# First output projection with three column groups over all token blocks and the fourth by pairs; the later modulation summed during it; gate rows made ahead

## The chip, the cores and the metric

The kernel runs on one core of one Trainium2 chip. The metric is the device time of one execution in microseconds (us); for the kernel before the change it is the median of three runs. TensorE does the matrix products (PE in the profile, PEld for its weight loads), VectorE (DVE) and ScalarE (ACT) the elementwise work, SyncE (SP) issues all DMA transfers from one queue in order.

## What is computed

Two layers over 512 tokens of width 2048, all float32. Each layer normalises, modulates with `1 + scale` and `shift`, mixes, normalises the mixer's output, scales it with `gate` and adds it to the stream. Shift, scale and gate come from one vector `c` through a large matrix product.

```python
for l in range(DEPTH):
    mod = sc @ ada_w[l] + ada_b[l]          # sc = silu(c); 2048 x 6144 per layer
    shift, scale, gate = mod[:, :D_MODEL], mod[:, D_MODEL:2 * D_MODEL], mod[:, 2 * D_MODEL:]
    h = modulate(rmsnorm(x, g_pre[l]), shift, scale)
    if l < N_A_LAYERS:
        y = mlstm_mixer(h, a_w_in[l], ..., a_w_out[l])
    else:
        if l == N_A_LAYERS:
            kmod = sc @ kv_ada_w + kv_ada_b
            hkv = modulate(rmsnorm(x, kv_g), kmod[:, :D_MODEL], kmod[:, D_MODEL:])
            kv = hkv @ kv_w
            ...
        y = band_attention_mixer(h, k_sh, v_sh, b_w_in[j], b_rel[j], b_w_out[j])
    x = x + gate[:, None, :] * rmsnorm(y, g_post[l])
```

## The kernel before

Everything is one Tile program, `hybrid_trunk`. It writes the work in program order; a scheduler that runs when the program is built sets each engine's order from priorities and its own estimate of times, and hands out the buffers of a pool as they come free in that order. Every engine and the SP queue then run strictly in the order so fixed. `tc.high_priority(AHEAD)` moves instructions ahead of program order, `pin` keeps instructions in program order among themselves.

**Products in three passes.** A float32 operand is split into a high part (ACT, a cast) and the rest (DVE, a subtraction), and each product is three matmuls (`mm3`, L280). Weights come as a stream of pieces that `stream` (L75) lists and `raw_load`/`wpiece` (L223, L232) load, 512 KB for a piece of 128 x 1024, and split on L213; three raw pieces and three split ones are held. `proj_b` (L299) takes pieces of two rows of blocks by 512 columns: with four token blocks a piece feeds 24 matmuls, with a pair of token blocks 12. Its argument `at` holds steps that are written into the program ahead of a given row of blocks.

**Layer 0, front (L816 to L949).** A loop over eight heads. The modulation that layer 0's gate and the key input need, 48 columns of blocks, is summed in the background of heads 0 to 2: `background(n)` (L743) sums what it loaded the time before on DVE (L507, 128 x 2048 elements, 1 MB of `adaT` each) and loads n more into two buffers (`ada_load`, L501). For head 0 it stands at rows 2, 4, 8, 10 and 14 of the value projection, for head 1 at 2, 6, 8 and 12, for head 2 after each of four projections. `gates` (L678) and `scores` (L785) are other DVE work of head 0. Each head's output goes to DRAM (`ysc`).

**Layer 0, output projection (L1100 to L1115).** `rows(g, ms, ...)` (L1065) multiplies by columns g of `a_w_out`: group 0 for all four token blocks, then groups 1 to 3 for token blocks 0 and 1, then groups 1 to 3 again for blocks 2 and 3, so that these weights are loaded and split twice. `evac` (L993) multiplies the result with a row of gates from `gate_row` (L989) and sums its squares (`sqy`). While the second pair runs, the first is finished: `residual(m)` (L1010) loads x (`xr`, four tiles of pool `tp`), adds, stores the new stream (`xsc`) and sums squares (`sqx`); `turned(pair, gs, use)` (L1030) scales (`xn`, DVE), transposes on TensorE (`ps_x`, L1046), copies (`xk`, ACT) and stores the turned stream (`nsc`); if `use` it also makes the key input from PSUM (`key_input`, L1022: one ACT operation, then a split). For the first pair `use` is False: the key input is made later, in group 3, from tiles loaded back (`kept`, L1056). In the background, `scale_sums` and `scale_load` (L1076, L1084) sum the shift and scale of layer 1, 32 columns of blocks in quarters of 512 elements (128 loads of 256 KB, four buffers). Pool `tp` has six tiles of 256 KB, pool `rp`, which holds the projection's results, twelve.

**Keys and values (L1118 to L1195).** `values` (L1118) first runs for the pair 0 on groups 0 and 1, with `residual(2)` and `residual(3)` written ahead of it, `scale_steps(4, 10)` in group 0 and `turned(1, ...)` in group 1, at rows 2, 6, 10 and 14; then for pair 1, with `input_sums`. Eight pairs of key tiles follow (`proj_s`), with the rest of the scale sums, then `values` for groups 2 and 3.

**Layer 1.** Attention (L1302 to L1332), then the output projection `b_w_out` (L1402): three groups for all token blocks, the last by pairs. The sixteen columns of layer 1's gate are summed here, in halves of 1024 elements: `gate_sums` (L1381) at eight steps, four loads of 512 KB and four sums each, with four buffers. Four times, `gate_part` turns four of the columns into gate rows (`gates_out`, L756, one TensorE transpose `ps_gg` each) and stores them; `gate_row` loads a row just before it is needed; group 0 is multiplied last (`gate_first`).

Of the kernel before, what the change touches and what calls it, by code (L numbers as in the profile page):

```python
# [9 lines left out]
F32 = mybir.dt.float32  # L10
# [64 lines left out]
def stream():  # L75
# [81 lines left out]
def hybrid_trunk(ctx, tc, xT, xN, c, adaT, cols, wst, wg, ext, kc, out):  # L157
# [658 lines left out]
    for h in range(NH):  # L816
# [4 lines left out]
        for i in range(4):  # L821
# [10 lines left out]
            if 1 < h <= HALF:  # L832
                background(2)
# [21 lines left out]
        if h < HALF:  # L855
            add_at(at, {k: lambda: background(2) for k in ((2, 4, 8, 10, 14) if h == 0 else (2, 6, 8, 12))})
# [103 lines left out]
    tp = tst.enter_context(pool("t2", bufs=6, side="right"))  # L960
# [28 lines left out]
    def gate_row(layer, g, gb=ssum):  # L989

        nc.sync.dma_start(gb, ggd[layer, 4 * g : 4 * g + 4, :].rearrange("k p -> (k p)").partition_broadcast(P))

    def evac(ps, m, g, dst, gated=True, later=None):  # L993
        if later is not None:
            later[m] = lambda: nc.vector.tensor_tensor(dst, ps, gb, op=ALU.mult)
        elif gated:
            nc.vector.tensor_tensor(dst, ps, gb, op=ALU.mult)
        else:
            nc.vector.tensor_copy(dst, ps)
# [30 lines left out]
    def turned(pair, gs, use):  # L1030
# [3 lines left out]
        for g in gs:  # L1034
# [5 lines left out]
            for kk in range(2):  # L1040
# [24 lines left out]
    def rows(g, ms, xs, at={}):  # L1065
# [7 lines left out]
    scale_cols = [(48 + i, j) for j in range(4) for i in range(2 * KT)]  # L1073
    scale_in, scQ = [], []

    def scale_sums():  # L1076

        for i, j, a in scale_in:
            pin(nc.vector.tensor_tensor_reduce(  # L1079
                a, a, scQ[j], 1.0, mod[:, i : i + 1] if j else col(CB + i), ALU.mult, ALU.add, mod[:, i : i + 1]  # L1080
            ))
        scale_in.clear()

    def scale_load():  # L1084

        for i, j in scale_cols[:2]:
            d = slice(j * S, (j + 1) * S)
            if len(scQ) == j:
                scQ.append(cp.tile([P, S], F32, tag="sc", name=f"scQ{j}", bufs=2))
                pin(nc.sync.dma_start(scQ[j], csc[0, d].partition_broadcast(P)))  # L1090
            a = cp.tile([P, S], F32, tag="adq", name=f"adq{i}_{j}", bufs=4)
            pin(nc.sync.dma_start(a, adaT[i, :, d]))
            scale_in.append((i, j, a))
        del scale_cols[:2]

    def scale_steps(*ks):
        at = {k: lambda: (scale_sums(), scale_load()) for k in ks}
        return at | {k + 2: scale_load for k in ks}

    gate_row(0, 0)  # L1100
    rows(0, range(4), y_tile, scale_steps(4, 10, 16, 22, 28))
    for pair, ms in enumerate(PAIRS):
        for g in range(1, 4):
            at = scale_steps(4, 12, 20, 28) if pair == 0 else {}
            if pair == 1 and g == 1:
                at = {2: lambda: residual(0), 4: lambda: residual(1)}
                at |= {20 + 4 * i: lambda i=i: turned(0, [i], False) for i in range(3)}
            if pair == 1 and g == 2:
                at = {2: lambda: turned(0, [3], False)}
            if pair == 1 and g == 3:  # L1110
                at = {k: lambda k=k: [key_input(i, kept(i, slice(0, 2 * P)), slice(0, 2 * P)) for i in range(k // 2 - 1, k // 2 + 1)] for k in range(2, 32, 4)}
            if pair == 1:
                add_at(at, scale_steps(*((8, 14), (6, 14, 22), (8, 20))[g - 1]))
            gate_row(0, g)
            rows(g, ms, ys, at)  # L1115
# [46 lines left out]
    for pair, ms in enumerate(PAIRS):  # L1162
        for g in range(2):
            turn = {2 + 4 * i: lambda i=i: turned(1, [i], True) for i in range(4)} if pair == 0 and g == 1 else {}
# [10 lines left out]
    for i in range(KT // 2):  # L1175
# [3 lines left out]
        if 0 < i < 7:  # L1179
            add_at(at, {1: lambda: (scale_sums(), scale_load()), 3: scale_load})  # L1180
        if i == 7:
            at[1] = lambda: (scale_sums(), amul_cols(2, 48 + KT, GPRE + KT))
# [3 lines left out]
    assert not scale_cols and not scale_in  # L1186
# [5 lines left out]
    for g in range(2, 4):  # L1192
        n = -(-ATT_PAIRS // 2)
        ks = [k for k in range((g - 2) * n, min((g - 1) * n, ATT_PAIRS))]
        values(g, range(4), {2 + 4 * i: input_sums for i, k in enumerate(ks)})  # L1195
# [175 lines left out]
    late, last = [], {}  # L1371
    gate_cols = [(80 + i, j) for i in [*range(4, KT), *range(4)] for j in range(2)]
    gate_in = []

    def gate_begin():
        late.append(op.tile([P, D], F32, tag="sc", name="scC", bufs=1))
        late.append(op.tile([P, S], F32, tag="gb", name="gb0", bufs=1))
        nc.sync.dma_start(late[0], csc.rearrange("a d -> (a d)").partition_broadcast(P))
        gate_sums()

    def gate_sums():  # L1381

        for a in gate_in:
            ada_sum(*a, tc.keep_in_program_order, late[0])
# [86 lines left out]
```

## Time and profile before

| what | us |
|---|---|
| median of three runs | 2764.67 |
| lowest and highest run | 2760.27, 2767.65 |
| the profiled execution's own time | 2763.39 |
| its span, first to last instruction | 2761.6 |
| mean granted TensorE clock in it | 0.998 of full speed |

The profile is one execution, in microseconds from the first instruction. "Busy" is the time in which an engine's instructions ran; a matmul's end is modelled and its record overlaps the next, so the pace of TensorE is read from the number of matmuls in a stretch. A row of waits names the waiting instruction, `<-`, what it waited for, the sum of the waits, their number and the longest one. A row of the timeline gives start, duration, engine, line, operation, written tile `<-` read tiles, count, and in brackets the idle time before it. `SPq` is the issue of a DMA on SyncE's queue. In windows each engine's busy time is followed by its number of instructions, and at the end stand the granted TensorE clock, the busy share of the 16 DMA engines and their rate.

### The profile page before, as it was taken

What the parts mean: (1) busy time and instruction counts of PE and PEld (TensorE: products, weight loads), DVE (VectorE), ACT (ScalarE), POOL (GpSimd) and SP (SyncE); (2) the same over time, 40 slices, a digit from 0 to 9 for tenths busy, and PEclk for the clock granted to TensorE, in tenths of its full rate; (3) what the DMA queues carried; (4) which work ended last, traced back from release to release, by engine and by line L of the source; (5) the groups of instructions that cost most, each with busy time, mean ns of one, the idle gap of its engine ahead of it and who ended that gap; (6) DMA issues with size and microseconds to landing.
All of it is one profiled execution on the core that took longest, in us unless ns stands there. A gap on an engine that the chain in (4) does not pass through costs nothing.

```text
span 2761.6 us, 45211 instructions
## 1 busy us (share of the span) xinstructions
PE 2730.8 (99%) x17554; PEld 2486.7 (90%) x17554; DVE 2327.1 (84%) x3822; ACT 1440.0 (52%) x2048; POOL 0.2 (0%) x4
## 2 busy tenths in 40 slices
PE   8999999999999999999999999999999999999998
PEld 6887888899999999999998888877998999999887
DVE  8977979999899899998988577667996798898666
ACT  4243623555556565565555344558435566666523
POOL 0000000000000000000000000000000000000000
PEclk9999999999999999999999999999999999999999
DMA  9756787333333333333338699998655544444697
GB/s 368 290 205 222 265 327 273 121 100 125 107 111 114 95 123 108 115 110 100 125 107 282 215 295 304 303 308 272 216 178 192 168 122 130 127 125 130 211 313 238
DMA packets 174802, 527.27 MB, mean 191 GB/s; under 512 B 18757, under 2 KB 34661, under 8 KB 163961
## 3 DMA queue, kind: packets, MB, share of 16 engines
q1 hardware_dynamic: 174586, 524.38, 56.7%
q8 instruction: 137, 2.24, 0.3%
q14 instruction: 79, 0.65, 0.1%
HBM read 490.69 MB, written 38.85 MB: 192 GB/s over the span
## 4 chain that ended last, share of the span: by engine, by line
PE 79%; DVE 9%; DMA 8%; issue 2%; ACT 1%; SPq 0%; DVEq 0%; ACTq 0%
PE ps_y L278 11%; PE ps_azo L278 5%; PE ps_czo L278 5%; PE ps_dzo L278 5%; DMA ada<-in_adaT 4%; PE ps_kv L278 4%; PE ps_az L278 3%; PE ps_cz L278 3%; PE ps_dz L278 3%; PE ps_l L278 3%; PE ps_bzo L278 3%; DVE wl L213 3%; PE ps_o L278 3%; PE ps_v L278 2%; DVE ada L507 2%
## 5 line engine op out<-in xcount | busy, mean ns | idle before, releaser
L213 ACT CAST wh<-wr 128x1024 fp32r<-128x1024 f32 (+1 forms) x560 | 579.6, 1037 | 531.2 <-PE ps_y L278 185.9
L213 DVE TENSOR_TENSOR wl<-wr,wh 128x1024 fp32r<-128x1024 f32 (+1 forms) x560 | 673.5, 1205 | 177.8 <-ACT wh L213 175.3
L278 PE MATMUL ps_y<-wh,y 128*128 128x512 f32 x1536 | 476.5, 390 | 0.0
L213 ACT CAST wsh<-ws 128x768 fp32r<-128x768 f32 (+1 forms) x272 | 222.5, 818 | 416.4 <-PE ps_az L278 123.2
L278 PEld LDWEIGHTS ps_y<-wh,y 128*128 128x128 f32 x1536 | 288.1, 188 | 59.3
L213 DVE TENSOR_TENSOR wsl<-ws,wsh 128x768 fp32r<-128x768 f32 (+1 forms) x272 | 254.4, 935 | 85.9 <-ACT wsh L213 82.7
L278 PE MATMUL ps_y<-wl,y 128*128 128x512 f32 x768 | 299.6, 390 | 0.1
L507 DVE CUSTOM_DVE_ANT_0 ada<-ada,scB,cl 128x2048 f32<-128x2048 f32 (+1 forms) x80 | 185.5, 2320 | 20.1 <-DMA ada<-in_adaT 19.9
L252 DVE TENSOR_TENSOR ws<-wr 128x512 f32<-128x512 f32 (+1 forms) x272 | 181.7, 673 | 2.7 <-DMA wr<-in_wst 2.6
L278 PEld LDWEIGHTS ps_y<-wl,y 128*128 128x128 f32 x768 | 144.2, 188 | 31.3 <-DVE wl L213 1.8
L278 PE MATMUL ps_kv<-wh,hkv 128*128 128x512 f32 x512 | 160.5, 393 | 0.0
L278 PE MATMUL ps_v<-wh,h 128*128 128x512 f32 x384 | 120.2, 390 | 0.0
L278 PEld LDWEIGHTS ps_kv<-wh,hkv 128*128 128x128 f32 x512 | 96.9, 190 | 19.9
L254 DVE TENSOR_TENSOR ws<-wr 128x256 f32<-128x256 f32 (+1 forms) x272 | 111.6, 415 | 2.7
L253 DVE TENSOR_TENSOR wr<-ws,wr 128x256 f32<-128x256 f32 (+1 forms) x272 | 111.2, 414 | 1.8
L278 PE MATMUL ps_kv<-wl,hkv 128*128 128x512 f32 x256 | 101.3, 396 | 2.3 <-DVE wl L213 2.3
L278 PE MATMUL ps_l<-h,wh 128*128 128x512 f32 x320 | 98.4, 390 | 0.0
L278 PEld LDWEIGHTS ps_v<-wh,h 128*128 128x128 f32 x384 | 72.0, 188 | 14.8
L278 PE MATMUL ps_azo<-h,wh 128*128 128x256 f32 (+1 forms) x404 | 82.1, 294 | 0.0
L278 PE MATMUL ps_v<-wl,h 128*128 128x512 f32 x192 | 75.0, 391 | 0.0
L1079 DVE CUSTOM_DVE_ANT_0 adq<-adq,scQ,mod 128x512 f32<-128x512 f32 x96 | 69.6, 747 | 5.8 <-DMA adq<-in_adaT 5.8
L278 PEld LDWEIGHTS ps_l<-h,wh 128*128 128x128 f32 x320 | 59.9, 188 | 12.7 <-ACT wh L213 0.3
(442 smaller groups left out, 7242.3 us busy)
## 6 DMA issues: line engine op xcount, KB each, us to landing
wr<-in_wst SPq DMA_DIRECT2D x530, 512.0 KB, 4.1
ada<-in_adaT SPq DMA_DIRECT2D x78, 1024.0 KB, 6.7
adq<-in_adaT SPq DMA_DIRECT2D x128, 256.0 KB, 5.1
ada<-in_adaT SPq DMA_DIRECT2D x36, 512.0 KB, 7.2
xt<-nsc SPq DMA_DIRECT2D x48, 256.0 KB, 4.6
wr<-in_wst SPq DMA_DIRECT2D x26, 384.0 KB, 3.2
yr<-ysc SPq DMA_DIRECT2D x28, 256.0 KB, 5.3
ysc<-zo SPq DMA_DIRECT2D x24, 256.0 KB
```

What stands on the lines that cost most here:

```text
L213: ins = nc.scalar.copy(hi, src), nc.vector.tensor_tensor(lo, src, hi.bitcast(F32), op=ALU.subtract)
L252: nc.vector.tensor_tensor(t[:, : 2 * w], r[:, w : 3 * w], r[:, : 2 * w], op=ALU.subtract)
L253: nc.vector.tensor_tensor(r[:, w : 2 * w], t[:, w : 2 * w], r[:, :w], op=ALU.add)
L254: nc.vector.tensor_tensor(t[:, 2 * w :], r[:, 3 * w :], r[:, w : 2 * w], op=ALU.subtract)
L278: return nc.tensor.matmul(ps, a, b, start=start, stop=stop)
L507: pin(nc.vector.tensor_tensor_reduce(c, c, (sc or scB)[:, j * w : (j + 1) * w], 1.0, mod[:, i : i + 1] if j else col(CB + i), ALU.mult, AL ...
L1079: pin(nc.vector.tensor_tensor_reduce(a, a, scQ[j], 1.0, mod[:, i : i + 1] if j else col(CB + i), ALU.mult, ALU.add, mod[:, i : i + 1]))
```

## The change

The first output projection goes through its column groups 0, 1 and 2 for all four token blocks, and only through group 3 by pairs, so that 80 pieces of weights are loaded and split where there were 112. The key input of pair 0 is made straight from PSUM in `turned`, as it was for pair 1, and the reload (`kept`) of that pair goes. All modulation of layer 1, gate columns too, is summed during this projection and the key tiles, in halves of 1024 elements, two loads of 512 KB and two sums a step, with two buffers: a step at every fourth row of group 0, at every second row but the last of groups 1 and 2, and at four rows of the first pair of group 3. The eight steps of the last projection and its four transposes go; one `gates_out` for all sixteen columns stands in `values` of group 2. Two results of pair 0 live in pool `tp`, which gets a seventh tile. In layer 0's front, head 0 has seven background steps in its value projection in place of five, head 1 three in place of four, and head 2 loads six columns in place of eight.

```diff
-    tile_b("a_w_out", 0, 32)
-    for _ in PAIRS:
-        for g in range(1, 4):
-            tile_b("a_w_out", g * 512, 32)
+    for g in (0, 1, 2, 3, 3):
+        tile_b("a_w_out", g * 512, 32)
...
             if 1 < h <= HALF:
-                background(2)
+                background(2 - i % 2)
...
-            add_at(at, {k: lambda: background(2) for k in ((2, 4, 8, 10, 14) if h == 0 else (2, 6, 8, 12))})
+            add_at(at, {k: lambda: background(2) for k in ((2, 4, 6, 8, 10, 12, 14) if h == 0 else (2, 6, 12))})
...
-    tp = tst.enter_context(pool("t2", bufs=6, side="right"))
+    tp = tst.enter_context(pool("t2", bufs=7, side="right"))
...
-                if use:
-                    for j in range(2):
-                        key_input(k + j, ps[:, j * 2 * P : (j + 1) * 2 * P], t)
+                for j in range(2):
+                    key_input(k + j, ps[:, j * 2 * P : (j + 1) * 2 * P], t)
...
-                yt[m].append(rp.tile([P, S], F32, tag="r", name=f"y{m}_{g}"))
+                yt[m].append((pl or rp).tile([P, S], F32, tag="t" if pl else "r", name=f"y{m}_{g}"))
...
+    cols_left = [(48 + i, j) for j in range(2) for i in range(2 * KT)] + [(80 + i, j) for j in range(2) for i in range(KT)]
+    halves, sc = [], [None, None]
+    def half_sums_step():
+        for i, j, a in halves:
+            pin(nc.vector.tensor_tensor_reduce(
+                a, a, sc[1], 1.0, mod[:, i : i + 1] if j else col(CB + i), ALU.mult, ALU.add, mod[:, i : i + 1]
+            ))
+        halves.clear()
+        for i, j in cols_left[:2]:
+            d = slice(j * 2 * S, (j + 1) * 2 * S)
+            if sc[0] != j:
+                sc[:] = j, cp.tile([P, 2 * S], F32, tag="sc", name=f"scH{i}_{j}")
+                pin(nc.sync.dma_start(sc[1], csc[0, d].partition_broadcast(P)))
+            a = cp.tile([P, 2 * S], F32, tag="adh", name=f"adh{i}_{j}", bufs=2)
+            pin(nc.sync.dma_start(a, adaT[i, :, d]))
+            halves.append((i, j, a))
+        del cols_left[:2]
...
     gate_row(0, 0)
-    rows(0, range(4), y_tile, scale_steps(4, 10, 16, 22, 28))
-    for pair, ms in enumerate(PAIRS):
-        for g in range(1, 4):
-            at = scale_steps(4, 12, 20, 28) if pair == 0 else {}
...
-            gate_row(0, g)
-            rows(g, ms, ys, at)
+    rows(0, range(4), y_tile, steps_at(*range(2, 32, 4)))
+    for g in (1, 2):
+        gate_row(0, g)
+        rows(g, range(4), ys, steps_at(*range(0, 30, 2)))
+    gate_row(0, 3)
+    rows(3, PAIRS[0], ys, steps_at(2, 10, 18, 26), tp)
+    at = {2: lambda: residual(0), 4: lambda: residual(1)}
+    at |= {14 + 4 * i: lambda i=i: turned(0, [i]) for i in range(4)}
+    rows(3, PAIRS[1], ys, at)
...
-            elif g == 0:
-                turn = scale_steps(4, 10)
...
+        if i == 0:
+            amul_cols(2, 48 + KT, GPRE + KT)
+        if 0 < i:
+            at[1] = half_sums_step
...
+        if g == 2:
+            steps[4] = lambda: gates_out(1, 0, KT, tp)
...
-    gate_steps = {
-        0: {10: gate_begin},
...
+            if pair != PAIRS[1]:
+                gate_row(1, g)
+                add_at(at, row_steps.get(g, {}))
```

More of the change, by code (lines that the diff above doesn't have):

```diff
@@ L1028, in key_input, with turned @@
         split(hkv[k][:, 0, t], hkv[k][:, 1, t], tmp)
-    def turned(pair, gs, use):
+    def turned(pair, gs):
         ms = PAIRS[pair]
@@ L1063, in hybrid_trunk, with rows @@
     yt = [[] for _ in range(4)]
-    def rows(g, ms, xs, at={}):
+    def rows(g, ms, xs, at={}, pl=None):
         ps = [newp(f"ps_y0_{g}_{m}") for m in ms]
@@ L1163, in hybrid_trunk @@
         for g in range(2):
-            turn = {2 + 4 * i: lambda i=i: turned(1, [i], True) for i in range(4)} if pair == 0 and g == 1 else {}
+            turn = {2 + 4 * i: lambda i=i: turned(1, [i]) for i in range(4)} if pair == 0 and g == 1 else {}
             if pair:
                 turn = {k: input_sums for k in (2, 6, 12)}
-            elif g == 0:
-                turn = scale_steps(4, 10)
             values(g, ms, turn)
@@ L1178, in hybrid_trunk @@
         at = {2: input_sums} if ready < KT // 2 else {}
[L1179 to L1182, printed above, removed]
+        if i == 0:
+            amul_cols(2, 48 + KT, GPRE + KT)
+        if 0 < i:
+            at[1] = half_sums_step
         assert ready == KEY_PAIRS[i]
@@ L1185, in hybrid_trunk @@
         nc.sync.dma_start(ksc[i].rearrange("p a t -> p (a t)"), z.rearrange("p a t -> p (a t)"))
-    assert not scale_cols and not scale_in
+    assert not cols_left and not halves
     zxst.close()
@@ L1194, in hybrid_trunk @@
         ks = [k for k in range((g - 2) * n, min((g - 1) * n, ATT_PAIRS))]
-        values(g, range(4), {2 + 4 * i: input_sums for i, k in enumerate(ks)})
+        steps = {2 + 4 * i: input_sums for i, k in enumerate(ks)}
+        if g == 2:
+            steps[4] = lambda: gates_out(1, 0, KT, tp)
+        values(g, range(4), steps)
     h2 = []
@@ L1369, in finish @@
             nc.sync.dma_start(out[m, :, g * S : (g + 1) * S], y)
[L1371 to L1384, printed above, removed]
[L1385 to L1401 removed]
+    last = {}
+    row_steps = {1: {12: lambda: fetch_x(0)}, 2: {4: lambda: fetch_x(1), 12: lambda: fetch_x(2)}, 3: {2: lambda: fetch_x(3)}}
     for g in range(4):
@@ L1410, in hybrid_trunk @@
                     yo[m].append(op.tile([P, S], F32, tag="o", name=f"yo{m}_{g}"))
-                    evac(p, m, g, yo[m][g], g > 0, last if g == 3 and pair == PAIRS[1] else None)
+                    evac(p, m, g, yo[m][g], last if g == 3 and pair == PAIRS[1] else None)
     finish(2)
```

49 lines of the change are left out of this document (5 added, 44 removed).

## Prediction

> **What bounds the kernel now.** I read the page first, then windows, waits, the chain of waits and the DMA issues of each stretch that the change touches.
>
> ```profile
> PE 2730.8 (99%) x17554; PEld 2486.7 (90%) x17554; DVE 2327.1 (84%) x3822; ACT 1440.0 (52%) x2048; POOL 0.2 (0%) x4
> L278 PE MATMUL ps_y<-wh,y 128*128 128x512 f32 x1536 | 476.5, 390 | 0.0
> ```
> ```profile
> 1485.69 158.72 PE ps_y L278 x700
> ```
> ```profile
> 1556.00:1690.00 134.00, 134.00 (x592) 110.95 (x592) 94.36 (x152) 55.05 (x64) 0.00 (x0) 1.00 0.88 286
> ...
> 2616.00:2709.00 93.00, 91.74 (x406) 75.27 (x405) 64.90 (x94) 22.65 (x35) 0.00 (x0) 1.00 0.82 288
> ```
>
> The records overlap (390 ns each), so the pace is what counts: the chain has 700 matmuls of the output projection in 158.72 us, 0.227 us each. At that pace a piece for four token blocks (24 matmuls) takes 5.44 us, for a pair (12) 2.72 us. From 1556 to 1690, with the pair that loads and splits every weight a second time, 592 matmuls stand in 134 us, 0.226 us each: full pace, though the DMA engines are 0.88 busy. TensorE is the bound, and the second split costs nothing there. The number of matmuls does not change, so only stretches in which TensorE falls behind its pace can give time, and a new one is the only way to lose it.
>
> **The weights.** Removed are 112 - 80 = 32 loads of 512 KB, casts and subtractions:
>
> ```profile
> L213 DVE TENSOR_TENSOR wl<-wr,wh 128x1024 fp32r<-128x1024 f32 x48 | 58.7, 1224 | 42.5 <-ACT wh L213 42.4
> ```
>
> 32 x 1.224 = 39 us of DVE, and as many casts on ACT. These 48 subtractions had 42.5 us of idle time ahead of them in the 134 us, so they are covered by TensorE. I take 0 for this part; nothing is late behind it but the matmuls themselves.
>
> **The hand-over from projection to values.** Here lies the largest loss of before.
>
> ```profile
> 1846.18 5.71 DMA xr<-in_xN
> ...
> 1853.07 5.38 DMA adq<-in_adaT
> ...
> 1858.48 0.75 DVE adq L1079
> ...
> 1859.35 0.50 DVE xn L1038
> ...
> 1859.89 1.54 PE ps_x L1046 x6
> 1861.43 3.41 PE ps_kv L278 x8
> 1864.84 0.85 PE ps_x L1046 x4
> 1865.69 2.77 PE ps_kv L278 x12
> ```
> ```profile
> 1859.89 1.54 PE L1046 MATMUL ps_x<-kcs,xn 128*128 128x128 f32 x6 [3.53 <-DVE xn L1038]
> ```
> ```profile
> 1717.68 1.03 PE L1046 MATMUL ps_x<-kcs,xn 128*128 128x128 f32 x8
> ```
>
> The transposes of `turned(1)` wait 3.53 us for `xn`, which waits on DVE behind a background sum whose load has not landed, and before that for the last `xr`. After the wait, 8 matmuls take 3.41 us and not 1.81: the clock is halved. The 5.80 us from 1859.89 to 1865.69 hold those 8 and 10 transposes, which at full pace (8 transposes in 0.8 to 1.0 us) are 2.8 us of work. So the place costs 3.5 + 3.0 = 6.5 us. The Trainium skill ("TensorE: Matmul & The Clock Gate", part 1) says that the clock falls to half after an idle window of some 3.4 us and rises after as long a busy one; the trace agrees (3.53 us idle, about 6 us slow). By that rule a wait below 3.4 us would cost only itself.
>
> ```profile
> 1826.03 0.42 SPq L1015 DMA_DIRECT2D xr<-in_xN  x1
> ...
> 1832.57 1.00 SPq L1092 DMA_DIRECT2D adq<-in_adaT  x2
> ...
> 1835.92 0.33 SPq L1019 DMA_DIRECT2D xsc<-y  x1
> ...
> 1846.18 0.43 SPq L1015 DMA_DIRECT2D xr<-in_xN  x1
> ...
> 1848.28 0.43 SPq L1015 DMA_DIRECT2D xr<-in_xN  x1
> ```
>
> The sixth of the eight `xr` is issued at 1826.03, the last two 20 us later: six tiles in `tp`, and in SP's queue the background loads and the stores of `xsc` between. After the change no background step stands in `values` of pair 0, the sum that made DVE wait for a 5.4 us load is gone, and a seventh tile takes a seventh `xr`. One `xr` stays late; if it is issued when the first tile comes free (the first `xsc` store, at 1835.92, follows that tile's reader), it is there some ten us earlier than now (1848.28), against 3.5 wanted. I take -6.5 us; the ends are 0 (the wait remains) and -6.5.
>
> But the first pair's hand-over becomes as tight. `residual(0)` and `(1)`, `turned(0)` and 16 key inputs now share the 16 pieces of group 3, pair 1 (43.5 us). ACT has there, by the durations of the same work for pair 1:
>
> ```profile
> L213 ACT CAST wh<-wr 128x1024 fp32r<-128x1024 f32 x33 | 34.6, 1049 | 16.8 <-DMA wr<-in_wst 11.7 <-PE ps_kv L278 4.7
> L1025 ACT ACTIVATE ps_x<-ps_x,mod,amul 128x256 f32<-128x256 f32 x16 | 8.3, 549 | 0.0
> L213 ACT CAST hkv<-ps_x 128x256 fp32r<-128x256 f32 x16 | 5.5, 397 | 0.1
> L1018 ACT ACTIVATE sqx<-y 128x512 f32<-128x512 f32 x8 | 4.8, 596 | 2.0 <-DVE y L1017 1.8
> L1050 ACT COPY xk<-ps_x 128x512 f32<-128x512 f32 x8 | 4.5, 591 | 5.0 <-PE ps_x L1046 3.5 <-DMA nsc<-xk 1.4
> ```
>
> 16 casts at 1.05 are 16.8 us, 16 x 0.549 = 8.8, 16 x 0.397 = 6.4, 8 x 0.596 = 4.8, 8 x 0.591 = 4.7: 41.5 of 43.5, with none of it possible before `residual` has begun. Some of it runs over into `values`, which wants the 16 key tiles one pair per 2.72 us, so the overrun has 20 us to drain. `turned(1)` did the same at the same spacing within eight pieces and TensorE kept its pace after 1865.69. I take 0 here; the range is a wait like the one above, up to +6.5. With `kept` for pair 0 go 16 loads; they made TensorE late by this much:
>
> ```profile
> PEld ps_y L278 <- DVE wl L213: 1.3, 4, 0.5
> ```
>
> Four weight loads, 1.3 us, partly beside running matmuls: I take -0.5 us (0 to -1.3).
>
> **The gate columns at the end.** In the last projection the transposes `ps_gg` wait in TensorE's order:
>
> ```profile
> PE ps_gg L763 <- DVE ggate L761: 1.3, 2, 1.0
> PE ps_gg L763 <- ACT sqy L1000: 1.2, 1, 1.2
> ```
>
> 2.5 us, all of which goes with the steps; the one transpose that remains stands in `values` of group 2, long after its last sum (the seventh key pair), beside other work. -2.5 us, ends -3 and -1.5. The sums themselves ran at full pace (406 records in 93 us, those waits among them).
>
> **The background loop, the cost of the change.** Groups 1 and 2 now sum two halves for each piece:
>
> ```profile
> L507 DVE CUSTOM_DVE_ANT_0 ada<-ada,scC,mod 128x1024 f32<-128x1024 f32 x16 | 20.5, 1283 | 10.0 <-DMA ada<-in_adaT 9.5
> ```
> ```profile
> wr<-in_wst SPq DMA_DIRECT2D x530, 512.0 KB, 4.1
> ...
> ada<-in_adaT SPq DMA_DIRECT2D x36, 512.0 KB, 7.2
> ```
> ```profile
> wr<-in_wst SPq DMA_DIRECT2D x4, 512.0 KB, 3.3
> ```
> ```profile
> wr<-in_wst SPq DMA_DIRECT2D x51, 512.0 KB, 4.8
> ```
> ```profile
> 1550.32 1.22 DVE L213 TENSOR_TENSOR wl<-wr,wh 128x1024 fp32r<-128x1024 f32 x1 [4.21 <-ACT wh L213]
> ```
>
> Work is no problem: 2 x 1.28 + 1.22 = 3.8 us of DVE in 5.44, and 1.57 MB in 5.44 us is 289 GB/s where 286 flowed (1556 to 1690). The latency is: with two buffers a load is issued when its sum ends and the next sum of that buffer waits until it lands. The period is 1.28 + about 0.2 (read-out and issue) + L. It exceeds 5.44 us if L is over 4.0 us. DVE then waits in order, and behind the waiting sum stands the subtraction of the next weights, and on SP the next loads behind the one that waits for the sum. The cover is that DVE subtracts three pieces ahead: in a stretch without background a subtraction starts at 1550.32 as soon as TensorE frees a piece and ends 8.6 us before TensorE wants it (two pieces of 5.44 us less the cast of 1.05 and 1.22). Two groups last 174 us and have 30 steps, so the price is 30 x (1.48 + L) - 174 - 8.6 where that is positive: 0 for L up to 4.6, 6 us for 4.8 and 20 us for 5.3. The rows for 512 KB are 3.3 us (1535 to 1556, nothing beside it), 4.1 (the median of all 530), 4.8 (1560 to 1700, at the same rate but with up to four quarters outstanding) and 7.2 (last projection, four halves issued together). Two halves 1.3 us apart and one piece of weights are fewer than in the last two rows, so I take the median, 4.1, and price 0; with jitter +1 us. Bounds 0 and, by 7.2, 30 x 8.68 - 183 = +78. "DMA: Bandwidth & Descriptors" of the Trainium skill (section on the anatomy of one DMA) fits 2.0 us plus bytes over 436 GB/s for one transfer of another path, an estimate of 3.2 us, near the 3.3 alone; by it this part would be 0 too.
>
> **The front.** Head 0 gets four more sums in its value projection, heads 1 and 2 two fewer each.
>
> ```profile
> 247.13 2.35 DVE L507 CUSTOM_DVE_ANT_0 ada<-ada,scB,cl 128x2048 f32<-128x2048 f32 x1 [1.14 <-DMA ada<-in_adaT]
> ...
> 256.87 2.35 DVE L507 CUSTOM_DVE_ANT_0 ada<-ada,scB,cl 128x2048 f32<-128x2048 f32 x1 [0.36 <-DMA ada<-in_adaT]
> ```
> ```profile
> ada<-in_adaT SPq DMA_DIRECT2D x6, 1024.0 KB, 8.1
> ```
> ```profile
> PE ps_q L278 <- ACT sp_q L213: 1.6, 1, 1.6
> PE ps_bzo L278 <- DVE p L807: 1.1, 1, 1.1
> ```
>
> Two buffers and 8.1 us to landing give two sums in 2.35 + 0.2 + 8.1 = 10.7 us, where seven steps of 5.44 us want two in each. Two steps more can so make DVE some 10 us later there; less the 8.6 us of cover that is up to +2, and 0 if the sums slip behind the weights. Against it, the columns end sooner, and two waits of TensorE, 2.7 us, at the end of head 1 and where head 2's tiles take over the background's memory, may shrink. I take 0, range -2.7 to +8.
>
> **The sum.** -6.5 - 0.5 - 2.5 + 1 + 0 = -8.5 us against the profiled execution's 2763.4 gives 2754.9. The median of the runs is 1.3 us above that execution, inside their spread of 7.4, so I say 2755. What a measurement here can tell from no change is 0.3%, 8.3 us: the forecast is just beyond it.
>
> **Rivals.** *The wait moves.* `turned(0)` stands 7 pieces (19 us) into group 3's second pair, and two of the seven tiles hold results until it is through; if its `xn` is late, the 6.5 us are paid there in place of at 1859. For it: five free tiles for eight `xr`. Against: no background loads are in that stretch. Sum without that term: 2761.4, within 0.3%. Chance 0.27.
>
> *The background starves DVE* (the other side): place, groups 1 and 2; price 20 us with L = 5.3; it decides from L = 4.6. For it: the 7.2 us of the last projection; against: 3.3 to 4.8 elsewhere. 2754.9 + 19 = 2774, slower. Chance 0.18.
>
> *The front's sums block* (+8, with the rest as forecast): 2763, within 0.3%. Chance 0.08.
>
> The forecast has 0.47, of which about 0.06 falls short of 0.3%; with 0.02 of the first rival that gains more, faster is 0.43, same 0.38 (0.06, 0.25 and 0.07 of the three), slower 0.19 (the second rival, and 0.01 of the third). Range: down to 2747, if both front waits go and the second values stretch gains as well; up to 2775, the starved loop. Below and above I leave about 0.1 each.
>
> **What would show it.** Right: no wait of `ps_x` over 1 us and a clock of 1.00 after the projection, no `ps_gg` wait in the last projection, 0.227 us for each matmul in groups 1 and 2. Wrong: DVE idle for `adh` loads in groups 1 and 2 with landings over 4.6 us and TensorE waiting for `wl`; a wait of `ps_x` in group 3's second pair; TensorE waits between 240 and 300 us.

## The result and the profile after

The changed kernel takes 2785.48 us (median of four runs, 2781.11 to 2791.59) against 2765.16 us for the kernel before on the same chip: a ratio of 1.0078, 95% interval 1.0056 to 1.0101. It is slower by 20 us, beyond the upper end of the forecast and on the other side of no change. The profiled execution has a span of 2781.8 us, 20.2 us more than before.

From the page of the changed kernel: engines, three groups (busy and mean time, then idle time of the engine ahead of them and what ended it) and two DMA issues with their median landing.

```profile
PE 2733.4 (98%) x17551; PEld 2485.8 (89%) x17551; DVE 2281.7 (82%) x3655; ACT 1402.9 (50%) x2011; POOL 0.2 (0%) x4
...
L276 PE MATMUL ps_y<-wh,y 128*128 128x512 f32 x1536 | 478.7, 392 | 13.2 <-ACT sqy L996 13.1
...
L1076 DVE CUSTOM_DVE_ANT_0 adh<-adh,scH,cl 128x1024 f32<-128x1024 f32 x48 | 61.4, 1283 | 52.4 <-DMA adh<-in_adaT 52.0
...
wr<-in_wst SPq DMA_DIRECT2D x498, 512.0 KB, 3.7
...
adh<-in_adaT SPq DMA_DIRECT2D x96, 512.0 KB, 4.8
```

Before, the 1536 matmuls of `ps_y` with `wh` had 0.0 us of idle time ahead of them; now they have 13.2. TensorE's waits over the whole changed kernel (sum, number, longest), the rows that matter here:

```profile
PE ps_y L276 <- ACT sqy L996: 13.1, 2, 7.1
PE ps_y L276 <- DVE wl L211: 7.9, 10, 1.3
PE ps_s L276 <- DVE e L800: 2.8, 1, 2.8
...
PE ps_dk L276 <- ACT hs L211: 2.3, 1, 2.3
PE ps_x L1042 <- DVE xn L1034: 2.0, 2, 1.3
```

And the changed kernel by windows (us, busy time of PE, PEld, DVE, ACT, POOL with their instructions, then clock, DMA share, GB/s): groups 1 and 2, the hand-over to the values, and the last projection.

```profile
1559.00:1660.00 101.00, 90.65 (x393) 73.01 (x392) 58.13 (x80) 18.13 (x20) 0.00 (x0) 0.98 0.70 241
1660.00:1761.00 101.00, 91.17 (x387) 73.59 (x388) 61.29 (x85) 21.03 (x29) 0.00 (x0) 0.96 0.77 252
...
1856.00:1915.00 59.00, 58.19 (x275) 47.08 (x274) 40.73 (x67) 47.63 (x97) 0.00 (x0) 1.00 0.89 295
2629.00:2730.00 101.00, 101.00 (x447) 83.61 (x447) 29.18 (x30) 25.93 (x40) 0.00 (x0) 1.00 0.45 146
```

In the two groups 780 matmuls stand in 202 us, 0.259 us each, where 0.227 was the pace. Neither DVE (59%) nor the DMA engines (0.70 and 0.77) are full, and the stretch of the kernel before that held full pace had the DMA engines busier (0.88). That is the picture of a latency: everybody waits, nobody works too much. DVE at the end of group 1, from its timeline in the changed kernel (start, duration, in brackets the idle time before):

```profile
1637.34 1.28 DVE L1076 CUSTOM_DVE_ANT_0 adh<-adh,scH,mod 128x1024 f32<-128x1024 f32 x1 [1.85 <-DMA adh<-in_adaT]
...
1643.34 1.29 DVE L1076 CUSTOM_DVE_ANT_0 adh<-adh,scH,mod 128x1024 f32<-128x1024 f32 x1 [1.75 <-DMA adh<-in_adaT]
...
1649.71 1.28 DVE L1076 CUSTOM_DVE_ANT_0 adh<-adh,scH,mod 128x1024 f32<-128x1024 f32 x1 [1.99 <-DMA adh<-in_adaT]
...
1656.96 1.28 DVE L1076 CUSTOM_DVE_ANT_0 adh<-adh,scH,mod 128x1024 f32<-128x1024 f32 x1 [3.00 <-DMA adh<-in_adaT]
1658.17 0.08 DVE L1076 DVE_READ_ACCUMULATOR2_ANT mod<- 128x1 f32 x1
1658.17 1.22 DVE L211 TENSOR_TENSOR wl<-wr,wh 128x1024 fp32r<-128x1024 f32 x1
1659.31 2.47 DVE L995 TENSOR_TENSOR y<-ps_y,ssum 128x512 f32<-128x512 f32 x4
```

The first two steps shown are 12.37 us for two, 6.2 us each: 1.48 + 4.75, the loop of the prediction with L = 4.75 (the median landing of `adh` is 4.8 us from 1560 to 1650 and 4.7 from 1650 to 1740). The last one, with a wait of 3.00, is 7.25. TensorE gives 5.44. Such a step of 6.2 falls 0.8 us further behind. TensorE's work on group 1 ends near 1653.6, but the evacuation (`y`, then `sqy` on ACT) stands in DVE's order behind the last sums and starts at 1659.31. Windows of the changed kernel around that place:

```profile
1653.50:1660.70 7.20, 0.12 (x1) 0.00 (x0) 4.20 (x8) 0.68 (x3) 0.00 (x0) 0.74 0.65 221
1660.70:1663.70 3.00, 2.94 (x7) 2.38 (x8) 3.00 (x5) 2.75 (x8) 0.00 (x0) 0.50 0.74 274
1663.70:1668.00 4.30, 4.30 (x20) 3.52 (x20) 1.63 (x3) 1.05 (x1) 0.00 (x0) 0.99 0.98 245
```

TensorE stands for 7.1 us; behind that its clock is 0.50 for 3.0 us, in which 7 matmuls start where 13 would, 1.4 us more. The same happens once more at the end of group 2 (the longer of the two waits is the 7.1, so the other is 6.0; behind it again 7 matmuls start in 3.0 us, from 1759.93). With the 7.9 us for `wl` (7.1 of them in groups 1 and 2, 0.8 in the first pair of group 3) the loop costs 13.1 + 7.9 + 2 x 1.4 = 23.8 us.

### The profile page after: what moved, and what is told of

Read it like the earlier page. It is cut to its first block, busy times and chain, and to the rows that moved or that the text cites. A ratio compares the mean times of both kernels' runs of the same rounds, so it can differ in the third digit from the quotient of the medians.

```text
span 2781.8 us, 44822 instructions
## 1 busy us (share of the span) xinstructions
PE 2733.4 (98%) x17551; PEld 2485.8 (89%) x17551; DVE 2281.7 (82%) x3655; ACT 1402.9 (50%) x2011; POOL 0.2 (0%) x4
## 4 chain that ended last, share of the span: by engine, by line
PE 81%; DMA 10%; DVE 5%; issue 2%; ACT 1%; SPq 0%; DVEq 0%; ACTq 0%
PE ps_y L276 10%; DMA adh<-in_adaT 6%; PE ps_azo L276 5%; PE ps_czo L276 5%; PE ps_dzo L276 5%; PE ps_kv L276 4%; PE ps_az L276 3%; PE ps_cz L276 3%; PE ps_dz L276 3%; PE ps_v L276 3%; PE ps_l L276 3%; PE ps_bzo L276 3%; PE ps_o L276 3%; PE ps_s L276 2%; PE ps_czq L276 2%
## 5 line engine op out<-in xcount | busy, mean ns | idle before, releaser
L211 ACT CAST wh<-wr 128x1024 fp32r<-128x1024 f32 (+1 forms) x528 | 545.7, 1036 | 590.0 <-PE ps_y L276 253.6
L211 DVE TENSOR_TENSOR wl<-wr,wh 128x1024 fp32r<-128x1024 f32 (+1 forms) x528 | 633.4, 1202 | 178.1 <-ACT wh L211 176.7
L276 PE MATMUL ps_y<-wh,y 128*128 128x512 f32 x1536 | 478.7, 392 | 13.2 <-ACT sqy L996 13.1
L1076 DVE CUSTOM_DVE_ANT_0 adh<-adh,scH,cl 128x1024 f32<-128x1024 f32 x48 | 61.4, 1283 | 52.4 <-DMA adh<-in_adaT 52.0
L1076 DVE CUSTOM_DVE_ANT_0 adh<-adh,scH,mod 128x1024 f32<-128x1024 f32 x48 | 61.6, 1283 | 45.7 <-DMA adh<-in_adaT 45.5
```

The costliest lines, as they stand in the source:

```text
L211: ins = nc.scalar.copy(hi, src), nc.vector.tensor_tensor(lo, src, hi.bitcast(F32), op=ALU.subtract)
L276: return nc.tensor.matmul(ps, a, b, start=start, stop=stop)
L1076: pin(nc.vector.tensor_tensor_reduce(a, a, sc[1], 1.0, mod[:, i : i + 1] if j else col(CB + i), ALU.mult, ALU.add, mod[:, i : i + 1]))
```

## Experiments

Theory A says that the landing time sets the pace, because each buffer goes round sum, issue, landing. Rival B says that the bytes are too many for the DMA engines. Rival C says that DVE's work and order (two sums a piece ahead of the subtraction and the evacuation) would cost the same whenever the data came. Ratios are to runs of the kernel before on the same chip (2761.6, 2761.6 and 2762.4 us in the three sets: the four kernels up to `e4`, the four up to `e9`, the last two).

| kernel | us | ratio, 95% interval |
|---|---|---|
| e1_resident: sums without loads | 2756.48 | 0.9984, 0.9975 to 0.9993 |
| e2_short: loads without sums | 2766.44 | 1.0017, 1.0007 to 1.0026 |
| e3_spread: the steps spread out | 2783.58 | 1.0084, 1.0070 to 1.0098 |
| e4_quarters5: five quarters, six tiles | 2754.64 | 0.9974, 0.9966 to 0.9983 |
| e6_quarters4: four quarters | 2772.35 | 1.0035, 1.0022 to 1.0048 |
| e7_back: two steps put back in the values | 2756.72 | 0.9981, 0.9972 to 0.9989 |
| e8_quarter_rows: five quarters, seven tiles | 2753.76 | 0.9967, 0.9956 to 0.9979 |
| e9_rows_front: e8 with the front of before | 2756.95 | 0.9979, 0.9971 to 0.9988 |
| e10_thirteen: 13 steps a group | 2767.23 | 1.0019, 1.0009 to 1.0028 |
| e5_tp6: six tiles | 2779.98 | 1.0060, 1.0046 to 1.0075 |

**Sums without loads.** In groups 1 and 2 `load` is False, and a sum whose tile is None reads one resident tile and writes a second; the 60 columns that belong there are left out.

```diff
+            if not load:
+                halves.append((i, j, None))
+                continue
             a = cp.tile([P, 2 * S], F32, tag="adh", name=f"adh{i}_{j}", bufs=2)
             pin(nc.sync.dma_start(a, adaT[i, :, d]))
```

> Groups 1 and 2 of the first output projection keep their 60 half sums, in number, size and place, but the sums read one tile that is loaded once, so that 59 of the 60 loads of 512 KB are gone (60 half columns are so not summed, and the output is not the reference's). Theory A (each of the two buffers is a loop of sum 1.28 us, 0.2 us and a landing of 4.75 us, so a step takes 6.2 us where TensorE gives it 5.44): DVE waits for no landing, the 98 us of idle time ahead of the sums go down to about 40, the waits of ps_y for sqy (13.1 us) and for wl (7.9 us) go, and with them the halved clock; 25 us less, 2760 us (2754 to 2766). Rival B (the bytes: 1.57 MB for each piece is more than the DMA engines give beside the weights): the same here, 2760. Rival C (DVE's work and order: two sums for each piece stand ahead of the subtraction and, at the end of a group, of the evacuation, whenever their data come): the work is the same, so 2780 to 2786, with the 13.1 us still there.

Measured 2756.48 us, 26 us less than the changed kernel by the ratios (1.0078 to 0.9984). Its windows of 90 and 95 us in groups 1 and 2, and its weight loads from 1560 to 1650:

```profile
1560.00:1650.00 90.00, 90.00 (x398) 74.51 (x397) 61.01 (x84) 21.62 (x31) 0.00 (x0) 1.00 0.36 118
1650.00:1745.00 95.00, 95.00 (x421) 78.65 (x420) 66.77 (x90) 23.06 (x30) 0.00 (x0) 1.00 0.38 122
```
```profile
wr<-in_wst SPq DMA_DIRECT2D x16, 512.0 KB, 3.4
```

All of DVE's work is there, 61 and 67 us of it, and TensorE runs at 0.226 us a matmul. The work and its order cost nothing: rival C falls. (A and B expected the same here.) The switch of the row of silu(c), a reload into the one buffer, is still in this kernel, and no wait of TensorE for `wl` or `sqy` follows it.

**Loads without sums.** In groups 1 and 2 `w` is 16, so each sum takes 16 of its 1024 elements.

```diff
-                a, a, sc[1], 1.0, mod[:, i : i + 1] if j else col(CB + i), ALU.mult, ALU.add, mod[:, i : i + 1]
+                a[:, :w], a[:, :w], sc[1][:, :w], 1.0, mod[:, i : i + 1] if j else col(CB + i), ALU.mult, ALU.add, mod[:, i : i + 1]
```

> All loads of the changed kernel stay, at their places, but in groups 1 and 2 each sum takes only the first 16 elements of its 1024 (the rest of these 60 half columns is left out of the modulation). A sum is then 0.1 us and not 1.28. Theory A: the loop is 0.1 + 0.2 + 4.75 = 5.05 us, below the 5.44 of a piece, so that the lag no longer adds up: the wait for sqy and most of the wait for wl go, 2760 us (2755 to 2768), though every byte is still moved and somewhat earlier. Rival B (bytes): the loads are as many and as large in the same stretch, so 2780 to 2786 and landings still of 4.75 us or more with DMA engines over 0.75 busy. Rival C (DVE's work and order): the work is gone, 2760 as well. With e1, A alone expects both cured.

Measured 2766.44 us, at the upper end of A's range and far below B's. The loads of 1560 to 1650 in that kernel, and its waits over the whole projection:

```profile
adh<-in_adaT SPq DMA_DIRECT2D x29, 512.0 KB, 5.4
wr<-in_wst SPq DMA_DIRECT2D x16, 512.0 KB, 5.5
```
```profile
PE ps_y L276 <- ACT sqy L996: 5.2, 2, 3.4
...
PE ps_y L276 <- DVE wl L211: 0.8, 1, 0.8
```

With the loads re-issued sooner they land later, 5.4 and not 4.75 us, and a short sum takes 0.23 us and not 0.1, so the loop is 0.23 + 0.2 + 5.4 = 5.83 us: still 0.4 above TensorE's 5.44, where the changed kernel's is 0.8 above. The two waits that are left are 1.8 us behind group 1 and 3.4 behind group 2, where they were 7.1 and 6.0. The expectation missed on L. A shorter loop leaves shorter waits, as A says; their size was not worked out beyond that.

**The steps spread out.**

```diff
+    SPREAD = [
+        (2, 4, 8, 10, 14, 16, 20, 22, 26, 28, 30),
+        (0, 2, 4, 6, 10, 12, 14, 16, 20, 22, 24, 26, 28),
+        (0, 2, 4, 8, 10, 12, 16, 18, 20, 24, 26, 28),
+        (2, 6, 12, 16, 22, 26),
+    ]
...
-        rows(g, range(4), ys, steps_at(*range(0, 30, 2)))
+        rows(g, range(4), ys, steps_at(*SPREAD[g]))
```

> All 96 half sums with two buffers, but the steps placed so that they come at most at 6.2 to 7.9 us on average: 11 in group 0 (before 8), 13 and 12 in groups 1 and 2 (15 and 15), 6 in the first pair of group 3 (4), 7 in the key product. Nothing else differs and the kernel computes all. Theory A: a group of 16 pieces is 87 us and 13 steps of 6.23 us take 81, so the lag never exceeds the cover of 8.6 us: waits for sqy below 2 us, for wl below 2 us, 2760 us (2755 to 2767). Rival B (bytes): 286 GB/s become about 260 in groups 1 and 2, and the bytes go to groups 0 and 3; a gain of half at most, 2772. Rival C (order): sums still stand at the last pieces of each group ahead of the evacuation, so the 13.1 us for sqy stay: 2775 to 2786.

Measured 2783.58 us: A's expectation failed, and the time lies in C's range, though the 13.1 us that C expected for `sqy` are 5.7. That wait, at the start of group 1, those of the transposes, and the DVE rows at the switch of the row in group 1:

```profile
PE ps_x L1042 <- DVE xn L1034: 7.1, 4, 4.8
PE ps_y L276 <- ACT sqy L996: 5.7, 1, 5.7
```
```profile
1604.42 1.22 DVE L211 TENSOR_TENSOR wl<-wr,wh 128x1024 fp32r<-128x1024 f32 x1
1610.96 1.28 DVE L1083 CUSTOM_DVE_ANT_0 adh<-adh,scH,mod 128x1024 f32<-128x1024 f32 x1 [5.32 <-DMA adh<-in_adaT]
```

The arithmetic of the expectation was short. Thirteen steps of 6.23 us are 81, but the three pieces without a step have their subtraction (3 x 1.22), and the switch stops DVE for 5.3 us: 90 us in a group of 87. Groups 0 and 1 also met in seven steps on end (rows 26, 28, 30, 0, 2, 4, 6), with an evacuation in the middle, and that is where the 5.7 us are. Another 7.9 us are for `wl`, as in the changed kernel, and the transposes wait 7.1 us (4.8 of them once, at the hand-over) where the changed kernel's wait 2.0; why was not tried. In neither of the two placements do 96 half sums with two buffers fit. After the fact this agrees with A, but it is no proof of it.

**Five quarters.**

```diff
-    tp = tst.enter_context(pool("t2", bufs=7, side="right"))
+    tp = tst.enter_context(pool("t2", bufs=6, side="right"))
...
-            a = cp.tile([P, 2 * S], F32, tag="adh", name=f"adh{i}_{j}", bufs=2)
-            pin(nc.sync.dma_start(a, adaT[i, :, d]))
+            a = cp.tile([P, S], F32, tag="adq", name=f"adq{i}_{j}_{q}", bufs=5)
+            pin(nc.sync.dma_start(a, adaT[i, :, j * 2 * S + q * S : j * 2 * S + (q + 1) * S]))
...
+        del cols_left[:4]
```

> The steps stay where the changed kernel has them (15 and 15 in groups 1 and 2), but each takes four quarters of 256 KB in place of two halves of 512 KB, in five buffers in place of two (for which the pool of temporary tiles goes from seven back to six). Same bytes, 0.4 us more of DVE's work in a step (four sums of 0.75 us). Theory A: a buffer comes round after 5 quarters, 1.25 pieces or 6.8 us, and needs 0.75 + 0.2 + about 4.5 = 5.5 us, so DVE keeps pace: no wait for sqy, 2762 us (2755 to 2768). Rival B (bytes): the same bytes in the same stretch with more of them outstanding, landings grow to over 5.5 us, 2780 or more. Rival C (work and order): DVE has more to do ahead of the evacuation, 2786 or more.

Measured 2754.64 us, just below A's range. Landings from 1560 to 1650 and the windows in this kernel:

```profile
adq<-in_adaT SPq DMA_DIRECT2D x63, 256.0 KB, 5.3
```
```profile
1560.00:1650.00 90.00, 90.00 (x399) 74.55 (x398) 67.08 (x147) 19.47 (x24) 0.00 (x0) 1.00 0.86 284
1650.00:1745.00 95.00, 95.00 (x421) 78.69 (x420) 72.11 (x153) 23.37 (x28) 0.00 (x0) 1.00 0.89 294
```

The same steps at the same places, more DVE work than in the changed kernel, and 284 and 294 GB/s where the changed kernel moved 241 and 252: TensorE has full pace. B falls with this: the bytes fit. So does C a second time. A buffer comes round after 6.8 us and needs 0.75 + 0.2 + 5.3 = 6.25, although the landing is longer than in the changed kernel.

**Four quarters.** The kernel above with `bufs=4` and seven tiles: the memory of the two halves.

```diff
-            a = cp.tile([P, S], F32, tag="adq", name=f"adq{i}_{j}_{q}", bufs=5)
+            a = cp.tile([P, S], F32, tag="adq", name=f"adq{i}_{j}_{q}", bufs=4)
```

> As the kernel with five quarters, but with four buffers of 256 KB (the memory of the changed kernel's two halves, and its seven temporary tiles). Theory A (each buffer is a loop of sum, 0.2 us and landing): a buffer must come round once for each piece, 0.75 + 0.2 + L in 5.44 us, so it decides from L = 4.5; with the 5.2 us that quarters took with five buffers the period is 6.15 us, as in the changed kernel: waits of ps_y for wl and sqy again, 2775 to 2786. Rival (what helped was the smaller tile, which lands sooner, and not the fifth buffer): L about 4.3, 2753 to 2758.

Measured 2772.35 us. Landings from 1560 to 1650, waits of TensorE in group 2 (1660 to 1770), and DVE at the switch of the row in group 1 and in group 2, in this kernel (its profile is of its fastest run, 2766.92 us):

```profile
adq<-in_adaT SPq DMA_DIRECT2D x60, 256.0 KB, 4.5
```
```profile
PE ps_y L276 <- ACT sqy L996: 5.5, 1, 5.5
PE ps_y L276 <- DVE wl L211: 3.7, 3, 1.6
```
```profile
1613.26 0.75 DVE L1077 CUSTOM_DVE_ANT_0 adq<-adq,scH,mod 128x512 f32<-128x512 f32 x1 [3.92 <-DMA adq<-in_adaT]
...
1710.99 0.75 DVE L1077 CUSTOM_DVE_ANT_0 adq<-adq,scH,cl 128x512 f32<-128x512 f32 x1 [3.69 <-DMA adq<-in_adaT]
```

L is 4.5 us, just the point from which the expectation had it decide: 0.75 + 0.2 + 4.5 = 5.45 us against 5.44. Group 1 pays 1.1 us of waits and group 2 pays 9.2, though the switch of the row stops DVE in both, for 3.92 and 3.69 us. So the switch alone does not explain group 2, and why it pays more stays open. Both sides of the expectation missed: quarters do land sooner with four outstanding than with five, yet not enough, and the fifth buffer is needed.

**Thirteen steps a group.** The last two steps of groups 1 and 2 go, and the last 8 of the 96 half columns are left out.

```diff
+    del cols_left[-8:]
...
-        rows(g, range(4), ys, steps_at(*range(0, 30, 2)))
+        rows(g, range(4), ys, steps_at(*range(0, 26, 2)))
```

> The changed kernel (two buffers of 512 KB) without the last two steps of groups 1 and 2: 13 steps at the first 13 pieces of each group, none at the last three (the last 8 of the 96 half columns are so left out of the sums). Theory A (each step takes 6.2 us where TensorE gives 5.44, so the lag grows by 0.8 us with each step and is paid where the evacuation stands behind the last sums): the lag at the thirteenth sum is 9 to 10 us, and three pieces without a sum give it back before the evacuation: the 13.1 us of waits for sqy go with the halved clock behind them, some waits for wl stay; 2762 us (2757 to 2769). Rival (bytes): the loads of the first 13 pieces are as dense as before, so most of the loss stays, 2775 or more.

Measured 2767.23 us, within A's range. The waits of the projection in this kernel:

```profile
PE ps_y L276 <- DVE wl L211: 7.8, 9, 1.7
...
PE ps_y L276 <- ACT sqy L996: 1.2, 1, 1.2
```

The wait for the evacuation goes from 13.1 to 1.2 us; that for `wl` stays. With the two stretches of halved clock (2.8 us) that is 14.7 us, and by the ratios (1.0078 to 1.0019) the kernel gains 16. So the dear part is the lag that the last steps carry to the group's end. The loads of the thirteen pieces that keep a step are as dense as before, so B misses here too.

**The best version, and its front.** Five quarters need 2 KB more; a quarter row of silu(c) in place of a half gives them back, and the seven tiles stay.

```diff
-    cols_left = [(48 + i, j) for j in range(2) for i in range(2 * KT)] + [(80 + i, j) for j in range(2) for i in range(KT)]
+    cols_left = [(48 + i, j) for j in range(4) for i in range(3 * KT)]
...
-                sc[:] = j, cp.tile([P, 2 * S], F32, tag="sc", name=f"scH{i}_{j}")
+                sc[:] = j, cp.tile([P, S], F32, tag="sc", name=f"scH{i}_{j}")
...
+            a = cp.tile([P, S], F32, tag="adq", name=f"adq{i}_{j}", bufs=5)
...
-        if i == 0:
-            amul_cols(2, 48 + KT, GPRE + KT)
...
+        if i == 7:
+            at[1] = lambda: (half_sums_step(), amul_cols(2, 48 + KT, GPRE + KT))
```

> The changed kernel with quarters in five buffers of 256 KB and one quarter row of silu(c) (2 KB in place of 4), the columns taken quarter by quarter over all 48, so that the seven temporary tiles stay. Theory A: a buffer has 6.8 us for 0.75 + 0.2 + 5.2, no wait for wl or sqy in groups 1 and 2, and with seven tiles the 3.2 us wait of ps_bk for the values' copy of the kernel with six goes too: 2750 us (2745 to 2756), 0.4% below the kernel before. Rival (each of the three switches of the row stops DVE for a landing, 5 us, as the row has one buffer): up to 3 x 5 us where the cover is used up, 2760 or more.

Measured 2753.76 us, ratio 0.9967 (0.9956 to 0.9979): 9 us less than before by the ratio, and within A's range. It is the lowest of all, though its interval overlaps that of five quarters with six tiles. Its first projection has no wait of TensorE, in spite of three switches of the row; landings are 5.1 us from 1560 to 1650 and 4.8 from 1650 to 1745, and in the latter the DMA engines are 0.85 busy:

```profile
1650.00:1745.00 95.00, 95.00 (x421) 78.67 (x420) 71.11 (x154) 22.24 (x29) 0.00 (x0) 1.00 0.85 291
```

Then the front alone was put back to that of the kernel before:

```diff
-                background(2 - i % 2)
+                background(2)
...
-            add_at(at, {k: lambda: background(2) for k in ((2, 4, 6, 8, 10, 12, 14) if h == 0 else (2, 6, 12))})
+            add_at(at, {k: lambda: background(2) for k in ((2, 4, 8, 10, 14) if h == 0 else (2, 6, 8, 12))})
```

> The kernel with quarter rows, with the three lines of the front (steps of heads 0, 1 and 2) as in the kernel before. The changed front has a wait of ps_s for e of 2.8 us near 266 us and lacks the waits of ps_q (1.6) and ps_bzo (1.1) of before. Theory (the two cancel): within 2 us of the kernel with quarter rows. Rival (the front's four sums more in head 0 cost 3 to 6 us with the halved clock): 3 to 6 us less than that kernel.

Measured 2756.95 us, 3.2 more than with the new front, where the expectation had at most 2 us of difference and the rival 3 to 6 less; the intervals overlap. Its waits from 150 to 560, and those of the best version there:

```profile
PE ps_n L276 <- DVE so L932: 5.1, 1, 5.1
PE ps_bzo L276 <- DVE p L805: 1.4, 1, 1.4
```
```profile
PE ps_n L276 <- DVE so L932: 3.1, 1, 3.1
PE ps_s L276 <- DVE e L800: 1.0, 1, 1.0
```

The two fronts wait for different things, and the same front waits 2.8 us for `e` in the changed kernel and 1.0 in the best version. No cost of the new front is resolved.

**The hand-over, two ways.** Six tiles in the changed kernel, then two background steps put back into the values of the best version.

```diff
-    tp = tst.enter_context(pool("t2", bufs=7, side="right"))
+    tp = tst.enter_context(pool("t2", bufs=6, side="right"))
```

> The changed kernel with six temporary tiles in place of seven, nothing else. The prediction counted on the seventh tile for an earlier last xr of the second pair's residual. If it matters, the wait of ps_x for xn at the hand-over comes back (3 us and the halved clock), 3 to 6 us more than the changed kernel, 2789 to 2791. Rival (the gone background step is what freed the hand-over): waits of ps_x as in the changed kernel (2.0 us), the same time within 2 us.

```diff
+            elif g == 0:
+                turn = steps_at(4, 10)
...
-        rows(g, range(4), ys, steps_at(*range(0, 30, 2)))
+        rows(g, range(4), ys, steps_at(*range(0, 30 if g == 1 else 26, 2)))
```

> The kernel with quarter rows (five buffers of 256 KB, seven temporary tiles), with two of its background steps put back to where the kernel before had them: from the end of group 2 into the first column group of the values, at its third and sixth piece, just ahead of the transposes of the second pair. Theory of the prediction (a sum whose load has not landed stands on DVE ahead of xn, and its loads on SP ahead of xr): TensorE waits for xn up to 3.5 us there and has the halved clock behind it, 2 to 6.5 us more than the kernel with quarter rows. Rival (the seventh tile alone cured the hand-over): the same time as that kernel, within 1.5 us.

Six tiles: 2779.98 us, not slower than the changed kernel (the intervals overlap), and in it the transposes of both pairs wait 1.5 us in all. The seventh tile is not what freed the hand-over. Two steps put back: 2756.72 us against 2753.76, which is 3 us more and so in the range of the theory, but with intervals that overlap. Waits of the kernel with the steps put back, 1820 to 1900, then the best version's:

```profile
PE ps_x L1042 <- DVE xn L1034: 2.3, 2, 1.4
```
```profile
PE ps_x L1042 <- DVE xn L1034: 0.7, 1, 0.7
```

The steps add 1.6 us of waits, not the whole 6.5, and no halved clock: with five buffers DVE is idle 0.1 us in all ahead of its eight sums there, where one sum of the kernel before waited 2.4 us for its load. How the rest divides between the late loads of that kernel and its late `xr` was not tried.

## Why the prediction was wrong

**The background loop: the step that failed.** The mechanism was in the text and was the rival "the background starves DVE"; its sign (DVE idle for `adh` in groups 1 and 2, landings over 4.6 us, TensorE waiting for `wl`) is what the profile shows. Two things made its price 0 in the sum.

First, L. I took 4.1 us, the median of all 530 weight loads of a kernel whose DMA engines are only some 0.3 busy in a third of its span, and set aside the 4.8 us of the same stretch in the kernel before. It was 4.75.

Second, the formula. With L = 4.8 it gives 6 us, not 24. It set one cover of 8.6 us, that of the weights, against 30 steps in a row. But there is a second thing behind the sums on DVE, the evacuation, and that has no cover: TensorE's next group needs the PSUM that `sqy` reads. So the lag of each group, 14 x 0.8 us, is paid at its end, above what the steps' places leave free; and behind both such waits, of 7.1 and 6.0 us, the clock was halved. I also left out the reload of the row of silu(c): in the changed kernel DVE stands 6.3 us at it in group 1, as this row of its timeline shows, and 4.8 us in group 2. What share of the lag is due to it was not tried; with five buffers three such switches cost TensorE nothing.

```profile
1622.72 1.28 DVE L1076 CUSTOM_DVE_ANT_0 adh<-adh,scH,mod 128x1024 f32<-128x1024 f32 x1 [6.31 <-DMA adh<-in_adaT]
```

The prediction cited "DMA: Bandwidth & Descriptors" of the Trainium skill (the anatomy of one DMA) for 3.2 us. The weight loads that run nearly alone in `e1_resident` agree (3.4 us); with the background beside them, the same 512 KB take 4.6 to 5.5, so an estimate from one transfer alone is the wrong one for a loop.

**The hand-over: right in size, half right in cause.** The 3.53 us wait and the clock of half speed behind it are gone (0.8 us of waits and a clock of 1.00 from 1856 to 1915). But the last two `xr` are as late as before: they are issued 9 us ahead of the transposes that need them, where it was 11.6 us in the kernel before. SP's rows in the changed kernel, then TensorE's at the hand-over:

```profile
1877.12 0.42 SPq L1011 DMA_DIRECT2D xr<-in_xN  x1
...
1884.17 0.53 SPq L1011 DMA_DIRECT2D xr<-in_xN  x1
1885.30 0.47 SPq L1011 DMA_DIRECT2D xr<-in_xN  x1
```
```profile
1894.45 0.87 PE L1042 MATMUL ps_x<-kcs,xn 128*128 128x128 f32 x6 [0.77 <-DVE xn L1034]
```

Seven tiles did not bring them forward, and six do no harm. "The wait moves" did not come true: group 3's second pair pays 1.3 us, where the second pair paid 0.7 before. By the granted clock the half speed in the kernel before lasted some 5 us (0.50 from 1859.8 to 1864.8), less than the 6 of the prediction, so its 3.0 us are rather 2.5.

**The last projection: right.** No wait of TensorE for `ps_gg` is left, and 447 matmuls stand in 101 us, 0.226 each. **The front: right as a zero.** The two waits of 1.6 and 1.1 us went, as the prediction said they might, and one of 2.8 us for `e` came; the clock stayed at 1.00 behind it (267 to 273 us). As that wait is 1.0 us in the best version with the same front, how much of it the front causes stays open. **Not foreseen:** the key tiles wait 2.3 us for `hs` and 1.2 for `wl`, and there are 0.7 us more beside them, where the values of the kernel before waited 2.3 us for `wl`. The zero for the weights and the -0.5 for the reload were not measured by themselves.

The sum as it came out: +23.8 (loop and clock), -2.5 (`ps_gg`), -5.9 (the hand-over, 2.9 us of waits and, as the prediction has it, 3.0 of clock gone), +0.6 (the first pair's wait), +0.1 (front), +1.9 (keys and values) = +18.0 us, against 20.2 in the spans; the other 2.2 us are not placed. Without the loop's term the forecast of -8.5 us stands as a total: the best version, which differs from the changed kernel in the buffers of that loop, the order of its columns and the place of `amul_cols`, is 9 us below the kernel before (6 to 12 by the interval). Its two large terms are as forecast: the waits of `ps_x` go from 4.4 to 0.7 us, the halved clock behind them is gone, and the 2.5 us for `ps_gg` too. The small terms do not match one by one, and in the changed kernel the terms other than the loop add up to -5.8 us, so that the totals are this near is in part luck.

## What to carry to other kernels

Price a background load as a loop: buffers divided by (work + issue + landing) must beat the consumer's pace with something over (here 6.8 us against 6.25 was enough, 5.44 against 5.45 was not), and the landing time must be that of the stretch with this very traffic: 4.5 us with four quarters outstanding was 5.3 with five. Then look at what else stands in the same engine's order: whatever has the least cover, here the evacuation at a group's end, pays for the whole lag. When engines and DMA are all part idle and the kernel is slow, try more buffers (smaller tiles, one more of them) before moving work: here they brought the whole loss back, and spreading the steps brought nothing.

## What was unexpected of the hardware

Half the size did not land in half the time: 512 KB in two buffers took 4.75 us, 256 KB in four took 4.5 and in five 5.3, and loads of 512 KB whose two buffers came free after a sum of 0.23 us took 5.4. The weights beside them shared it: 3.4 us with hardly anything else, 4.6 to 5.5 with the background. So size alone did not set the landing time; whether the number outstanding or the rate of the traffic did, these runs do not separate. Behind idle times of 7.1 and 6.0 us TensorE's clock was halved for 3.0 us, behind 3.53 us in the kernel before for some 5 us. The rule of the Trainium skill that the prediction cites ("TensorE: Matmul & The Clock Gate", part 1) agrees on the halving; the stretches until the clock rose lie on both sides of its 3.4 us.
